# A two-layer fp32 decoder on one core: late weight columns and norm sums moved to VectorE, memsets, accumulating DMAs and casts queued elsewhere, two weight columns kept

## The chip, the cores and the metric

One core of a Trainium2 chip runs one launch of the kernel. The metric is the device time of that launch in microseconds. Lower is better. The kernel before was timed in three runs.

## What is computed

Two post-norm decoder layers over T = 528 tokens (16 learned ones ahead of 512 real ones), width 1024, hidden width 2816, all in float32. Cut to what matters:

```python
def hybrid_layer(h, ...):
    proj = einsum('bld,de->ble', h, w_in)
    ...                       # retention, multi-scale pooling, forgetting attention
    mix = concatenate([o_r, o_p, o_f], axis=-1)
    h = layer_norm(ALPHA * h + einsum('ble,ed->bld', mix, w_out), ln1_g, ln1_b)
    a, b = einsum('bld,df->blf', h, w1), einsum('bld,df->blf', h, w3)
    y = einsum('blf,fd->bld', silu(a) * b, w2)
    return layer_norm(ALPHA * h + y, ln2_g, ln2_b)
```

This is done twice, after a layer norm of the embedded input. There are thus two norms per layer; the text calls those after w_out the mixing norms (m0, m1 for layers 0 and 1) and the one after w2 of layer 0 the FFN norm (f0).

## The kernel before, in words

**Numbers.** Activations lie transposed, as 8 tiles of 128 features by tokens, and are cut by tokens into half A (272) and half B (256). Each float32 value is used as a rounded part `hi` and a rest `lo`, and a product is three matmuls into one PSUM accumulator: hi·hi, hi·lo, lo·hi (`mm3`, L236 to L240). There are two such accumulators (`acc`), so a matmul group can start when the group two before it has been read out of PSUM.

**Weights.** A chunk of 128x1024 is loaded by SP into one of 3 `raw` buffers (L167), cast to its hi part on ScalarE (L184), and its lo part is raw minus hi, by `sub_lo` (L141) on VectorE or on GpSimd (POOL). `ensure` (L174) does this; which engine does the subtraction is set chunk by chunk where `add_chunks` is called, by the table `CFG`: `o0` to `o7` for the eight column groups of w_out (each is streamed once for half A and once for half B), `i*` for w_in, `n*` for the first chunks of the FFN. L141 is also the line of every other hi/lo subtraction (the rest `xl` of the activations among them), so in the trace tiles tell them apart.

**Order.** TensorE's order is written by hand: `Plan` places pieces of matmuls by priorities and by a table `LAG` of latencies. The order of the other engines' queues comes from a scheduler; `tc.issue_after(ins)` puts what is issued inside it behind the instruction `ins` on its engine. Every queue is in order: an instruction that waits holds up all behind it.

**Norm** (L318 to about L400, `Norm`). `evac` adds the residual to a PSUM result (L332, VectorE), adds it to a running sum (L337), squares it (L341, ScalarE; the last one on VectorE, L339) and adds the square to a second running sum (L345). `CFG` s1 to s7 and t1 to t7 choose VectorE or POOL for the sums of L337 and L345. `stats` has TensorE transpose the sums (L359) and VectorE reduce them (L360); some small steps (L366 to L369, the power on POOL) give each token's scale, and L372 writes it into a diagonal matrix g. `apply` has TensorE spread g over partitions (L376), then, per tile of 128 features, VectorE subtracts the mean (L381) and multiplies by the scale (L382), ScalarE applies gain and bias (L312) and casts to `xh` (L314), and POOL subtracts to `xl` (L141). The first products after a norm take these tiles one by one. While one half is normed, TensorE works on the other half's last columns.

**FFN.** The first three hidden tiles are plain products (`ffn_hidden`: SiLU on ScalarE at L1164, times the second product on VectorE at L1186 in the first layer and L1243 in the last). The others use a seven-product scheme (`fast`), which needs sums of weight blocks and of activation blocks. `sums_of` (L191) makes the former: one SP load, two DMAs from POOL's queue that add on arrival (L197 into `s`, L198 into `raw`), two adds on VectorE (L207, L210) and casts. Its casts and VectorE work are placed behind marks set in the apply step; its two POOL DMAs are not. `factors` and `sums_of_x` (L1026 to L1064) make the latter into `Th` and `Tl`, with casts on ScalarE (L1043).

**w2 of layer 0** is used in two halves of the hidden width. In the second half, columns 4, 5 and 6 are used for half A first and loaded, cast and split a second time for half B, in the order 6, 5, 4 (`M2`).

**Mixing.** At the start of each mixing stage `clear` (L564) zeroes the states, and `forget` calls `causal` (L631), which writes the attention mask; all on POOL (L566 to L571, L634, L635).

## Time and profile before

| | |
|---|---|
| median of 3 runs | 1247.58 us (1243.88 to 1247.93) |
| the profiled execution | 1246.58 us |
| its span | 1244.8 us, 23626 instructions |
| DMA | 153.34 MB, mean 123 GB/s |

The span is the time between the first and the last instruction of the profiled execution; the execution's own time is 1.8 us more. Busy time is per engine: PE is TensorE's matmuls, PEld its weight loads, DVE VectorE, ACT ScalarE, POOL GpSimd. PEclk is the clock TensorE was granted as a share of 2.4 GHz; 0.50 is its lower level, 1.2 GHz. In a timeline, a row is start, duration, engine, line, operation, out<-in, shape and count, and in brackets how long the engine had been idle and what ended that. Where like instructions follow one another on an engine, one row holds them with their count, and its time runs from the first one's start to the last one's end.

### The profile page before, as it was taken

What the parts mean: (1) busy time and instruction counts of PE and PEld (TensorE: products, weight loads), DVE (VectorE), ACT (ScalarE), POOL (GpSimd) and SP (SyncE); (2) the same over time, 40 slices, a digit from 0 to 9 for tenths busy, and PEclk for the clock granted to TensorE, in tenths of its full rate; (3) what the DMA queues carried; (4) which work ended last, traced back from release to release, by engine and by line L of the source; (5) the groups of instructions that cost most, each with busy time, mean ns of one, the idle gap of its engine ahead of it and who ended that gap; (6) DMA issues with size and microseconds to landing.
All of it is one profiled execution on the core that took longest, in us unless ns stands there. A gap on an engine that the chain in (4) does not pass through costs nothing. (4 is left out here: it accounts for less than half of the span.)

```text
span 1244.8 us, 23626 instructions
## 1 busy us (share of the span) xinstructions
PE 1193.6 (96%) x9154; PEld 1142.3 (92%) x9154; DVE 844.5 (68%) x1732; ACT 603.7 (49%) x1182; POOL 374.9 (30%) x417
## 2 busy tenths in 40 slices
PE   7999999889999999999989899999999999999996
PEld 6999989879999999999989799998899999998885
DVE  6575687899885268864674755779887777762327
ACT  5436554456563246653354265444655555552221
POOL 5423348650110011101264243386511111100004
PEclk9999999999999999999989999998999999999999
DMA  6331212454862367722443221124468777633221
GB/s 236 114 102 64 70 35 68 153 144 119 212 165 82 102 189 182 178 77 78 128 149 125 82 73 56 48 86 152 136 160 205 176 187 177 156 102 102 85 101 68
DMA packets 59520, 153.34 MB, mean 123 GB/s; under 512 B 8392, under 2 KB 17128, under 8 KB 59408
## 3 DMA queue, kind: packets, MB, share of 16 engines
q1 hardware_dynamic: 48464, 131.90, 33.2%
q0 software_dynamic: 10944, 19.93, 9.9%
q8 instruction: 72, 1.18, 0.4%
q14 instruction: 40, 0.33, 0.1%
HBM read 145.83 MB, written 2.10 MB: 119 GB/s over the span
## 5 line engine op out<-in xcount | busy, mean ns | idle before, releaser
L238 PE MATMUL acc<-xh,w 128*128 128x256 f32 (+1 forms) x1024 | 303.0, 296 | 11.4 <-DVE ka L141 5.0
L239 PE MATMUL acc<-xl,w 128*128 128x256 f32 (+1 forms) x1024 | 294.4, 288 | 5.4 <-POOL xl L141 4.7
L240 PE MATMUL acc<-xh,w 128*128 128x256 f32 (+1 forms) x1024 | 293.7, 287 | 0.0
L141 DVE TENSOR_TENSOR w<-raw,w 128x1024 fp32r<-128x1024 f32 (+3 forms) x234 | 225.7, 984 | 67.4 <-ACT w L184 63.5
L184 ACT CAST w<-raw 128x1024 fp32r<-128x1024 f32 (+1 forms) x184 | 182.5, 993 | 163.1 <-PE acc L240 104.0
L238 PEld LDWEIGHTS acc<-xh,w 128*128 128x128 f32 x1024 | 196.8, 192 | 16.0 <-issue 6.1
L239 PEld LDWEIGHTS acc<-xl,w 128*128 128x128 f32 x1024 | 197.0, 192 | 7.5 <-POOL xl L141 6.3
L240 PEld LDWEIGHTS acc<-xh,w 128*128 128x128 f32 x1024 | 196.6, 192 | 0.0
L141 POOL TENSOR_TENSOR w<-raw,w 128x256 fp32r<-128x256 f32 (+1 forms) x70 | 111.3, 1595 | 76.4 <-ACT w L184 70.1
L198 POOL DMA_DIRECT2D raw<-in_w x38 | 32.8, 864 | 329.0 <-DMA raw<-in_w 102.9
L1141 PE MATMUL acc<-xh,w 128*128 128x264 f32 (+1 forms) x608 | 121.8, 283 | 0.0
L1141 PEld LDWEIGHTS acc<-xh,w 128*128 128x128 f32 x608 | 98.6, 188 | 0.2 <-ACT g L1099 0.2
L1141 PE MATMUL acc<-xl,w 128*128 128x264 f32 (+1 forms) x304 | 85.4, 281 | 0.0
L141 DVE TENSOR_TENSOR S<-sr,S 128x512 fp32r<-128x512 f32 x76 | 52.4, 689 | 47.3 <-ACT S L209 46.6
L299 POOL TENSOR_TENSOR r<-r,mhalf 128x1 f32<-128x1 f32 (+3 forms) x18 | 14.7, 821 | 185.4 <-DVE r L298 185.4
L1141 PE MATMUL acc<-Th,w 128*128 128x264 f32 (+1 forms) x304 | 61.2, 284 | 0.0
L1141 PE MATMUL one<-Th,S 128*128 128x264 f32 (+1 forms) x304 | 61.1, 283 | 0.0
L1141 PE MATMUL one<-xh,S 128*128 128x264 f32 (+1 forms) x304 | 60.9, 283 | 0.0
L1141 PE MATMUL acc<-Th,S 128*128 128x264 f32 (+1 forms) x304 | 60.9, 283 | 0.0
L1141 PE MATMUL one<-xh,w 128*128 128x264 f32 (+1 forms) x304 | 60.2, 282 | 0.0
L1141 PEld LDWEIGHTS acc<-xl,w 128*128 128x128 f32 x304 | 57.2, 188 | 0.0
L197 POOL DMA_DIRECT2D s<-in_w x38 | 37.8, 1002 | 61.5 <-DVE g L1243 12.3
(492 smaller groups left out, 3139.3 us busy)
## 6 DMA issues: line engine op xcount, KB each, us to landing
raw<-in_w SPq DMA_DIRECT2D x88, 512.0 KB, 4.1
raw<-in_w_in SPq DMA_DIRECT2D x42, 512.0 KB, 4.1
raw<-in_w_out SPq DMA_DIRECT2D x32, 512.0 KB, 3.4
raw<-in_w2b SPq DMA_DIRECT2D x22, 512.0 KB, 3.5
s<-in_w SPq DMA_DIRECT2D x38, 256.0 KB, 3.7
s<-in_w POOLq DMA_DIRECT2D x38, 256.0 KB, 6.4
raw<-in_w POOLq DMA_DIRECT2D x38, 256.0 KB, 5.4
raw<-in_w2a SPq DMA_DIRECT2D x19, 512.0 KB, 3.5
```

The costliest lines, as they stand in the source:

```text
L141: return eng.tensor_tensor(lo, full, hi.bitcast(F32), op=ALU.subtract)
L184: nc.scalar.copy(w[:, 0, :n], raw[:, :n])
L197: nc.gpsimd.dma_start(r1, src2[:, b], accum_op=ALU.add)
L198: nc.gpsimd.dma_start(a2[:, a], src1[:, a], accum_op=ALU.add)
L238: nc.tensor.matmul(ps, lhsT=wh, rhs=hi, start=first, stop=False)
L239: nc.tensor.matmul(ps, lhsT=wh, rhs=lo, start=False, stop=False)
L240: nc.tensor.matmul(ps, lhsT=wl, rhs=hi, start=False, stop=last)
L299: nc.gpsimd.tensor_tensor(r[:np_, :nb], r[:np_, :nb], mhalf[:np_, :nb], op=ALU.pow)
L1141: nc.tensor.matmul(ps, lhsT=a[:, w], rhs=b, start=fresh and k == 0 and q == 0, stop=k == 3 and q == 2, skip_group_check=True)
```

## The change

1. **w_out.** The lo part of a chunk is now made on POOL only for half A's columns with `o*` set except the last (0, 1, 3, 4, 6) and for columns 3 and 4 of half B. Column 7 of half A and columns 0, 1, 6 and 7 of half B go to VectorE: five subtractions per layer.
2. **Sums.** `s1`, `s5`, `t1` and `t4` of `CFG` go from 1 to 0, so every running sum is on VectorE: 4 additions per half of each norm, 24 in all.
3. **Queues.** A new helper `behind` places instructions behind the latest apply step's last mark on VectorE ("v"), ScalarE ("s") or, newly, POOL ("p", the last `xl`). Behind "p" come the memsets of `clear` and the mask of `causal` (in layer 1; in layer 0 there is no mark yet); behind all three the whole of `sums_of`, its POOL DMAs included; behind "s" the casts to `Th`.
4. **Plan.** `LAG` T goes from 16 to 4, and the sums of activations depend on other pieces.
5. **w2.** In the second half of the hidden width, the split columns 5 and 6 are kept (tile `wheld`, in the place of `Th` and `Tl`, which are free by then) and used again for half B; only column 4 is loaded a second time. That takes away four SP loads (1.44 MB), four casts and four subtractions.

The lines of `LAG` and `CFG` are left out of the diff.

```diff
-M2 = (0, 1, 2, 3, 4, 5, 6, 7, 6, 5, 4)
...
@@ -175,11 +174,16 @@
         while len(loaded) < len(chunks) and len(loaded) <= upto:
             fetch(len(loaded))
             raw, (_, n, eng) = raws[len(loaded)], chunks[len(loaded)]
-            w = wp.tile([P, 2, 1024], F32R, tag="w", name="w")
+            if eng in ("Th", "Tl"):
+                if n == 1024:
+                    wf[eng] = wf["pool"].tile([P, 2, KH * P], F32R, tag=eng, name="wheld")
+                w, eng = wf[eng][:, :, 1024 * (n < 1024):], nc.vector
+            else:
+                w = wp.tile([P, 2, 1024], F32R, tag="w", name="w")
             if eng == "S2":
                 c = len(loaded)
-                with ExitStack() as gates:
-                    loaded.append(sums_of(raws[c - 1], raw, loaded[-1], w, chunks[c - 1][0], chunks[c][0], gates))
+                with behind("v", "s", "p"):
+                    loaded.append(sums_of(raws[c - 1], raw, loaded[-1], w, chunks[c - 1][0], chunks[c][0]))
                 continue
             nc.scalar.copy(w[:, 0, :n], raw[:, :n])
             if eng != "S1":
@@ -188,7 +192,7 @@
                         sub_lo(e, w[:, 1, c0:c1], raw[:, c0:c1], w[:, 0, c0:c1])
             loaded.append(w)
 
-    def sums_of(a1, a2, w1, w2, src1, src2, gates):
+    def sums_of(a1, a2, w1, w2, src1, src2):
 
 
         a, b = slice(0, 512), slice(512, 1024)
@@ -200,8 +204,6 @@
         s1, s2 = (wf["pool"].tile([P, 2, 512], F32R, tag="S", name="S", bufs=3) for i in range(2))
         s4 = wf["pool"].tile([P, 2, 512], F32R, tag="S4", name="S4", bufs=2)
         v = nc.vector
-        for e in "vs":
-            gates.enter_context(tc.issue_after(marks["apply", e].ins))
         sub_lo(v, w1[:, 1, a], a1[:, a], w1[:, 0, a])
         nc.scalar.copy(s1[:, 0], r1)
         v.tensor_tensor(r2, r1, a1[:, a], op=ALU.add)
@@ -221,7 +223,7 @@
     for l in range(DEPTH):
         win_u.append([add_chunks(d["w_in"][l, m], 1024, quarters if l == 0 and m < CFG["pw"] else (None, nc.gpsimd, nc.vector)[CFG[f"i{m}"]] if l and m < 4 else None)
                       for m in range(N_IN)])
-        wout_u.append({h: [add_chunks(d["w_out"][l, m], 1024, nc.gpsimd if CFG[f"o{m}"] else nc.vector)
+        wout_u.append({h: [add_chunks(d["w_out"][l, m], 1024, nc.gpsimd if CFG[f"o{m}"] and m != 7 and (h == "A" or m in (3, 4)) else nc.vector)
                            for m in range(KD)] for h in "AB"})
         w13_u.append([])
         for fs, cut in ((KH, slice(0, KH * P)), (KF, slice(KH * P, DFF))):
@@ -229,7 +231,8 @@
                 w13_u[l].append(add_chunks(d["w13"][l, f], 1024, f"S{1 + f % 2}" if f >= 2 * HEAD else
                                            nc.gpsimd if f < 4 and CFG[f"n{f}"] else nc.vector))
             if l < DEPTH - 1:
-                w2_u.append([add_chunks(d["w2a"][m][:, cut], KH * P, nc.vector) for m in M2[:KD if fs < KF else None]])
+                w2_u.append([add_chunks(d["w2a"][m][:, cut], KH * P, f"T{'hl'[m - 5]}" if m in (5, 6) and fs == KF else nc.vector)
+                             for m in (*range(KD), 4)[:KD if fs < KF else None]])
         if l == DEPTH - 1:
             w2_u.append([add_chunks(d["w2b"][k], 1024, nc.vector) for k in range(KF)])
 
@@ -312,8 +315,16 @@
         nc.scalar.activation(out=y, in_=y if src is None else src, func=AF.Identity,
                              scale=pv[:, gc:gc + 1], bias=pv[:, bc:bc + 1])
         ins = nc.scalar.copy(x[0], y)
-        sub_lo(nc.gpsimd, x[1], y, x[0])
+        marks["apply", "p"] = sub_lo(nc.gpsimd, x[1], y, x[0])
         return ins
+
+    def behind(*engines):
+
+        st = ExitStack()
+        for e in engines:
+            if ("apply", e) in marks:
+                st.enter_context(tc.issue_after(marks["apply", e].ins))
+        return st
 
     class Norm:
 
@@ -562,13 +573,14 @@
         state = [ap_.tile([P, 2, 192], F32, tag=f"state{i}", name=f"state{i}") for i in range(2)]
 
         def clear():
-            for t in state:
-                nc.gpsimd.memset(t, 0.0)
-            nc.gpsimd.memset(vbd, 0.0)
-            for t in qb:
-                nc.gpsimd.memset(t[64:66].bitcast(F32), 1.0)
-            for m in range(2):
-                nc.gpsimd.memset(pu[m][:, :NM], 0.0)
+            with behind("p"):
+                for t in state:
+                    nc.gpsimd.memset(t, 0.0)
+                nc.gpsimd.memset(vbd, 0.0)
+                for t in qb:
+                    nc.gpsimd.memset(t[64:66].bitcast(F32), 1.0)
+                for m in range(2):
+                    nc.gpsimd.memset(pu[m][:, :NM], 0.0)
 
         vraw = {}
 
@@ -643,7 +655,8 @@
             nc.scalar.activation(out=a, in_=a, func=AF.Exp, scale=-1.0)
             nc.scalar.activation(out=a, in_=a, func=AF.Ln, bias=1.0)
             nc.vector.tensor_scalar(b, fl, 0.0, None, op0=ALU.min)
-            causal()
+            with behind("p"):
+                causal()
             nc.vector.tensor_tensor_scan(fl, a, b, 0.0, op0=ALU.add, op1=ALU.subtract)
             for i in range(2):
                 F["c", i] = ap_.tile([6, T], F32R, tag="tmp", name="flp", bufs=7)
@@ -1040,7 +1053,8 @@
         for (p, c0, c1), (q, _, _) in zip(second(k), second(k + 4)):
             v.tensor_tensor(t[2][:, c0:c1], q, p, op=ALU.subtract)
         for i in range(3):
-            nc.scalar.copy(Th[:, k, i], t[i])
+            with behind("s"):
+                nc.scalar.copy(Th[:, k, i], t[i])
             sub_lo(v, Tl[:, k, i], t[i], Th[:, k, i])
 
         def fourth():
@@ -1059,9 +1073,9 @@
         def make(k):
             later[k] = factors(k, n, hs, o, Th, Tl)
 
-        ps = [plan.add(lambda k=k: make(k), 0.0, [units[k // 2], ready], 5) for k in range(4)]
+        ps = [plan.add(lambda k=k: make(k), 0.0, [units[k], ready], 5) for k in range(4)]
         end = plan.add(lambda: [later[k]() for k in range(4)], 0.0, ps + [units[-1]], 5)
-        ps[0].holds("y", 3, units[3])
+        ps[0].holds("y", 3, ps[-1])
         return [(ps[-1], LAG["T"]), end]
 
     PRODUCTS = dict(P1=("A11", "B11", 0), P5=("s1", "T1", 1), P6=("s2", "T2", 0), P7=("s3", "T3", 0), P2=("A12", "B21", 2),
@@ -1173,8 +1187,8 @@
         base = 16 + l * PV_L
         N = T // 2
         wf["pool"] = gp
-        Th = gp.tile([P, 4, 3, N], F32R, name="Th")
-        Tl = gp.tile([P, 4, 3, N], F32R, name="Tl")
+        Th = gp.tile([P, 4, 3, N], F32R, tag="Th", name="Th")
+        Tl = gp.tile([P, 4, 3, N], F32R, tag="Tl", name="Tl")
         gt = {}
 
         def split(f, c0, c1, t):
@@ -1200,7 +1214,7 @@
         for f in range(HEAD):
             for h in "AB":
                 done[(f, 0), h].holds("y", 1, done[(f, 1), h])
-        deps = sums_of_x(N, hs, 0, Th, Tl, [done[u, "B"] for _, u in us], ready["B", KD - 1][0])
+        deps = sums_of_x(N, hs, 0, Th, Tl, [done[us[i][1], h] for i, h in ((0, "B"), (0, "B"), (4, "A"), (4, "B"), (5, "B"))], ready["B", KD - 1][0])
         gdone = {f: [(done[(f, 1), h], LAG["g"]) for h in "AB"] for f in range(HEAD)}
         prev = done[us[-1][1], "B"]
         dn = {}
@@ -1216,16 +1230,20 @@
             last = fast(l, fs[0 if i else HEAD:], 0, N, Th, Tl, yslot, lambda f: (yslot(N), yslot(N)), gated, deps, prev)
             gdone.update({f: [(p, LAG["g2"])] for f, p in last.items()})
             end = [last[fs[-1]]]
-            us = list(zip(w2_u[i], M2))
+            us = list(zip(w2_u[i], (*range(KD), 4)))
+            if i:
+                us[8:] = us[6], us[5], us[8]
             for part, halves in ((us[:4], "AB"), (us[4:7], "A"), (us[7:8], "AB"), (us[8:], "B")) if i else ((us, "AB"),):
                 dn.update(stage(part, lambda half, fs=fs: {f: tuple(g[:, :NA] if half == "A" else g[:, NA:] for g in gt[f]) for f in fs},
                                 list(fs), lambda h, key: n_of[h],
                                 lambda m, half, ps, i=i: norm[half].evac(m, ps) if i else evac2(m, half, ps),
                                 lambda half, key, k, end=end: gdone[k] + end, halves=halves, ahead=1 if i else 2, k0=fs[0]))
+                if len(part) == 1:
+                    plan.add(lambda: ensure(w2_u[1][8][1]), 0.0, [dn[7, "B"]], 8)
             end = [dn[us[-1][1], h] for h in "AB"]
         xn, nready = {}, {}
         for half in "AB":
-            ap = norm[half].finish([dn[m, half] for m in (range(KD) if half == "A" else M2[:4] + M2[7:])], base + 16, base + 24, xn)
+            ap = norm[half].finish([dn[m, half] for m in (range(KD) if half == "A" else (0, 1, 2, 3, 7, 6, 5, 4))], base + 16, base + 24, xn)
             ap.append(plan.add(lambda half=half: free(keep[half]), 0.0, [ap[-1]], 0))
             for k in range(KD):
                 nready[half, k] = (ap[-2], norm[half].lag["ap"] + 0.85 * k)
@@ -1248,7 +1266,7 @@
         for f in range(HEAD):
             for h in "AB":
                 done[(f, 0), h].holds("y", 1, done[(f, 1), h])
-        deps = sums_of_x(NB, hw, NM, Th, Tl, [done[u, "B"] for _, u in us], ready["B", KD - 1][0])
+        deps = sums_of_x(NB, hw, NM, Th, Tl, [done[us[i][1], h] for i, h in ((0, "B"), (0, "B"), (4, "A"), (4, "B"), (5, "B"))], ready["B", KD - 1][0])
         last = fast(l, range(HEAD, KF), NM, NB, Th, Tl, yslot, lambda f: (g[f][:, :NB], g[f][:, NB:]), lambda f, j, g: None, deps, done[us[-1][1], "B"])
         ht = {}
```

TensorE's queue holds the same matmuls in the same order as before, save that some read `wheld`. VectorE has 30 instructions more, POOL 34 fewer, ScalarE and SP 4 fewer each.

**Place 1: VectorE at the norm of half A after w_out, layer 0.** Here `w<-raw,w` is the lo part of a w_out chunk and the rows with `c_ident` write the diagonal. Before:

```order
L141 TENSOR_TENSOR w<-raw,w 128x1024
L372 TENSOR_SCALAR y<-c_ident,r 128x16
L372 TENSOR_SCALAR y<-c_ident,r 128x128 x2
L381 TENSOR_TENSOR y<-y,one 128x272 x2
L332 SCALAR_TENSOR_TENSOR y<-y,acc 128x256
L337 TENSOR_TENSOR y<-y 128x256
L382 TENSOR_TENSOR y<-y,one 128x272
```

And now:

```order
L140 TENSOR_TENSOR w<-raw,w 128x1024
L383 TENSOR_SCALAR y<-c_ident,r 128x16
L383 TENSOR_SCALAR y<-c_ident,r 128x128 x2
L348 TENSOR_TENSOR y<-y 128x256
L392 TENSOR_TENSOR y<-y,one 128x272 x2
L356 TENSOR_TENSOR y<-y 128x256
L343 SCALAR_TENSOR_TENSOR y<-y,acc 128x256
L140 TENSOR_TENSOR w<-raw,w 128x1024
L393 TENSOR_TENSOR y<-y,one 128x272 x2
```

What stands ahead of the diagonal is the same; behind it there are two running sums and a w_out subtraction that POOL did before. From the diagonal to the last multiplication by the scale, VectorE now has four w_out subtractions (before none) and four more running sums.

**Place 2: ScalarE and VectorE at the first hidden tiles after that norm, layer 0.** `Th` are the casts of activation sums, L1164 (now L1178) is the SiLU; L1186 (now L1200) is the product that reads an accumulator. ScalarE before, then now:

```order
L1164 ACTIVATE y<-acc 128x256
L1043 CAST Th<-y 128x264 x4
L184 CAST w<-raw 128x1024
L1043 CAST Th<-y 128x264 x2
L1182 CAST g0h<-y 128x256
L184 CAST w<-raw 128x1024
L1043 CAST Th<-y 128x264 x2
L1164 ACTIVATE y<-acc 128x256
```

```order
L1178 ACTIVATE y<-acc 128x256
L1057 CAST Th<-y 128x264 x4
L188 CAST w<-raw 128x1024
L1057 CAST Th<-y 128x264 x2
L1178 ACTIVATE y<-acc 128x256
```

The second SiLU of half B stood behind eight casts of `Th` and stands behind six now. VectorE before, then now, in the same place:

```order
L382 TENSOR_TENSOR y<-y,one 128x256 x2
L207 TENSOR_TENSOR sr<-s_3782,raw 128x512
L210 TENSOR_TENSOR sr<-sr,raw 128x512
L1186 TENSOR_TENSOR y<-y,acc 128x272
L141 TENSOR_TENSOR g1l<-y,g1h 128x272
```

```order
L393 TENSOR_TENSOR y<-y,one 128x256 x2
L1200 TENSOR_TENSOR y<-y,acc 128x272
L140 TENSOR_TENSOR g1l<-y,g1h 128x272
...
L140 TENSOR_TENSOR Tl<-y,Th 128x264
L209 TENSOR_TENSOR sr<-s_3782,raw 128x512
L1200 TENSOR_TENSOR y<-y,acc 128x256
```

The weight sum L207 (now L209) no longer stands ahead of half A's product; it stands directly ahead of the next product of half B.

**Place 3: POOL at the norm of half A after w2, layer 0.** Before, then now:

```order
L141 TENSOR_TENSOR xl<-y,xh 128x272 x4
L141 TENSOR_TENSOR w<-raw,w 128x256
L566 MEMSET state_7848 128x384
L566 MEMSET state_7849 128x384
L567 MEMSET vbd 96x384
L569 MEMSET qb_7838 2x256
L569 MEMSET qb_7839 2x256
L141 TENSOR_TENSOR xl<-y,xh 128x272
L571 MEMSET pu_7844 128x16
L571 MEMSET pu_7845 128x16
L634 MEMSET mask 128x528
L141 TENSOR_TENSOR w<-raw,w 128x256
```

```order
L380 TENSOR_TENSOR r<-r,mhalf 128x3
L140 TENSOR_TENSOR w<-raw,w 128x256
L140 TENSOR_TENSOR xl<-y,xh 128x272 x6
L140 TENSOR_TENSOR w<-raw,w 128x256
L140 TENSOR_TENSOR xl<-y,xh 128x272 x2
L380 TENSOR_TENSOR r<-r,mhalf 128x2
L601 TENSOR_TENSOR y<-y,rcs 128x272
L140 TENSOR_TENSOR xl<-y,xh 128x256 x8
L578 MEMSET state_7826 128x384
```

The memsets and the mask stood between the subtractions of `xl`; now they follow the last `xl` of half B, and two quarter chunks of w_in stand among half A's eight.

## Rows read from the trace of the kernel before

**Rows 1.** The page, busy time of the engines.

```profile
PE 1193.6 (96%) x9154; PEld 1142.3 (92%) x9154; DVE 844.5 (68%) x1732; ACT 603.7 (49%) x1182; POOL 374.9 (30%) x417
```

**Rows 2.** Windows: stretch, length, busy per engine (instructions), PEclk, DMA share, GB/s.

```profile
220.00:300.00 80.00, 69.83 (x529) 67.55 (x528) 71.37 (x142) 41.99 (x83) 38.53 (x34) 0.96 0.44 132
300.00:620.00 320.00, 320.00 (x2621) 319.79 (x2621) 209.29 (x382) 152.38 (x279) 39.28 (x42) 1.00 0.53 139
620.00:645.00 25.00, 20.25 (x139) 19.31 (x139) 19.03 (x37) 13.10 (x25) 17.08 (x23) 0.86 0.64 210
850.00:915.00 65.00, 56.96 (x433) 55.43 (x432) 55.22 (x112) 33.67 (x69) 31.42 (x30) 0.92 0.48 138
242.84:246.25 3.41, 3.41 (x17) 3.30 (x16) 3.06 (x10) 2.03 (x5) 0.77 (x1) 0.50 0.49 154
908.44:911.85 3.41, 3.41 (x18) 3.41 (x17) 2.79 (x9) 0.38 (x1) 0.00 (x0) 0.50 0.57 127
200.00:260.00 60.00, 56.13 (x433) 55.05 (x432) 52.71 (x76) 33.29 (x58) 45.32 (x34) 0.97 0.41 137
```

**Rows 3.** TensorE's waits, 220 to 300: us in total, times, longest.

```profile
PE one L376 <- DVE y L372: 5.4, 2, 3.4
PE acc L238 <- DVE y L1186: 2.5, 1, 2.5
PE acc L238 <- ACT y L1164: 1.4, 1, 1.4
```

**Rows 4.** TensorE's waits, 620 to 645.

```profile
PE acc L239 <- POOL xl L141: 4.7, 3, 2.2
```

**Rows 5.** TensorE's waits, 850 to 915.

```profile
PE one L376 <- DVE y L372: 4.4, 2, 2.8
PE acc L238 <- ACT y L1164: 2.5, 1, 2.5
PE one L359 <- DVE y L345: 1.2, 1, 1.2
```

**Rows 6.** Timeline of VectorE, 219 to 262.

```profile
219.72 0.43 DVE L345 TENSOR_TENSOR y<-y 128x272 f32<-128x272 f32 x1
...
229.34 2.55 DVE L345 TENSOR_TENSOR y<-y 128x272 f32<-128x272 f32 x1
...
237.95 1.23 DVE L141 TENSOR_TENSOR w<-raw,w 128x1024 fp32r<-128x1024 f32 x1 [1.47 <-ACT w L184]
239.09 3.24 DVE L372 TENSOR_SCALAR y<-c_ident,r 128x16 f32<-128x16 f32 x3
...
251.98 0.78 DVE L382 TENSOR_TENSOR y<-y,one 128x272 f32<-128x272 f32 x2
```

**Rows 7.** Timeline of POOL, 229 to 261.

```profile
229.21 2.38 POOL L141 TENSOR_TENSOR w<-raw,w 128x1024 fp32r<-128x1024 f32 x1 [2.19 <-ACT w L184]
...
239.72 2.33 POOL L141 TENSOR_TENSOR w<-raw,w 128x1024 fp32r<-128x1024 f32 x1
...
257.51 2.79 POOL L141 TENSOR_TENSOR xl<-y,xh 128x272 fp32r<-128x272 f32 x3
```

**Rows 8.** All runs of line L372: ns of one, minimum, median, maximum.

```profile
L372 DVE TENSOR_SCALAR y<-c_ident,r x14: 234/284/2434, 239.1 to 885.3; 128x128 f32<-128x128 f32 x12, 128x16 f32<-128x16 f32 x2
```

**Rows 9.** Timeline of POOL, 629 to 637.

```profile
633.80 1.47 POOL L141 TENSOR_TENSOR xl<-y,xh 128x272 fp32r<-128x272 f32 x1
635.23 1.27 POOL L635 TENSOR_SCALAR_AFFINE_SELECT mask<-mask 128x128 f32<-128x128 f32 x1
```

**Rows 10.** Timeline of VectorE, 272 to 280.

```profile
273.02 5.67 DVE L207 TENSOR_TENSOR sr<-s,raw 128x512 f32<-128x512 f32 x1
```

**Rows 11.** Timeline of POOL, 272 to 280.

```profile
272.29 5.84 POOL L141 TENSOR_TENSOR xl<-y,xh 128x256 fp32r<-128x256 f32 x8
```

**Rows 12.** Timeline of ScalarE, 274 to 276.

```profile
274.65 0.70 ACT L314 CAST xh<-y 128x256 fp32r<-128x256 f32 x2
```

**Rows 13.** Tile s, 255 to 310: the adding DMAs' landing.

```profile
DMA to landing us min/median/max: 5.1/7.7/8.1
```

More of the change, by code (lines that the diff above doesn't have):

```diff
@@ L35 @@
 PV_L = 40
-LAG = dict(T=16.0, g2=3.0, y2=2.0, q=1.5, kb=4.25, fb=3.21, q_1=1.5, kb_1=5.0, fb_1=3.45, rot=8.62, vt=2.86, kt=3.84, kv=1.23, kvo=2.5, rs=2.5, ro=6.35, rp=0.69, f=12.8, a=5.62, b=0.77, v0=9.72, k=3.2, s=0.99, p=2.78, pt=1.24, mt=2.77, u=5.1, rm=3.74, pm=3.74, mx=3.25, y=0.8, st=2.25, ap=2.42, g=2.1, ga=8.46, gn=6.42, gt=21.89, gs=0.33, gs2=0.86, gl=2.0, w=10.8, rot_1=10.43, vt_1=1.2, kt_1=6.88, kv_1=0.74, kvo_1=1.6, rs_1=4.5, ro_1=7.28, rp_1=0.48, f_1=11.9, k_1=1.95, s_1=1.7, p_1=2.78, pt_1=1.16, mt_1=2.85, u_1=6.42, rm_1=3.0, pm_1=3.72, mx_1=3.17, y_m0A=0.8, y2_m0A=4.1, st_m0A=5.7, ap_m0A=2.42, y_m0B=1.6, y2_m0B=2.5, st_m0B=2.2, ap_m0B=2.42, y_f0A=0.8, y2_f0A=2.0, st_f0A=3.75, ap_f0A=2.42, y_f0B=2.5, y2_f0B=3.5, st_f0B=3.52, ap_f0B=2.42, y_m1A=0.8, y2_m1A=4.2, st_m1A=5.5, ap_m1A=2.42, y_m1B=1.6, y2_m1B=2.5, st_m1B=2.2, ap_m1B=3.15)
@@ L39 @@
-CFG = dict(h0=2, h1=1, h2=0, h3=2, h4=1, h5=2, h6=1, h7=2, g0=2, g1=1, g2=0, g3=0, g4=0, g5=2, g6=2, g7=1, p0=1, p1=0, p2=0, p3=0, p4=0, p5=0, p6=0, p7=0, q0=0, q1=1, q2=0, q3=1, q4=0, q5=1, q6=0, q7=1, pw=2, a3=7, a4=5, e1=7, e2=7, ws=1, wf=0, i0=2, i1=0, i2=0, i3=2, o0=1, o1=1, o2=0, o3=1, o4=1, o5=0, o6=1, o7=1, n0=0, n1=0, n2=0, n3=0, s1=1, s2=0, s3=0, s4=0, s5=1, s6=0, s7=0, t1=1, t2=0, t3=0, t4=1, t5=0, t6=0, t7=0)
+LAG = dict(T=4.0, g2=3.0, y2=2.0, q=1.5, kb=4.25, fb=3.21, q_1=1.5, kb_1=5.0, fb_1=3.45, rot=8.62, vt=2.86, kt=3.84, kv=1.23, kvo=2.5, rs=2.5, ro=6.35, rp=0.69, f=12.8, a=5.62, b=0.77, v0=9.72, k=3.2, s=0.99, p=2.78, pt=1.24, mt=2.77, u=5.1, rm=3.74, pm=3.74, mx=3.25, y=0.8, st=2.25, ap=2.42, g=2.1, ga=8.46, gn=6.42, gt=21.89, gs=0.33, gs2=0.86, gl=2.0, w=10.8, rot_1=10.43, vt_1=1.2, kt_1=6.88, kv_1=0.74, kvo_1=1.6, rs_1=4.5, ro_1=7.28, rp_1=0.48, f_1=11.9, k_1=1.95, s_1=1.7, p_1=2.78, pt_1=1.16, mt_1=2.85, u_1=6.42, rm_1=3.0, pm_1=3.72, mx_1=3.17, y_m0A=0.8, y2_m0A=4.1, st_m0A=5.7, ap_m0A=2.42, y_m0B=1.6, y2_m0B=2.5, st_m0B=2.2, ap_m0B=2.42, y_f0A=0.8, y2_f0A=2.0, st_f0A=3.75, ap_f0A=2.42, y_f0B=2.5, y2_f0B=3.5, st_f0B=3.52, ap_f0B=2.42, y_m1A=0.8, y2_m1A=4.2, st_m1A=5.5, ap_m1A=2.42, y_m1B=1.6, y2_m1B=2.5, st_m1B=2.2, ap_m1B=3.15)
@@ L42, in mix_half @@
+CFG = dict(h0=2, h1=1, h2=0, h3=2, h4=1, h5=2, h6=1, h7=2, g0=2, g1=1, g2=0, g3=0, g4=0, g5=2, g6=2, g7=1, p0=1, p1=0, p2=0, p3=0, p4=0, p5=0, p6=0, p7=0, q0=0, q1=1, q2=0, q3=1, q4=0, q5=1, q6=0, q7=1, pw=2, a3=7, a4=5, e1=7, e2=7, ws=1, wf=0, i0=2, i1=0, i2=0, i3=2, o0=1, o1=1, o2=0, o3=1, o4=1, o5=0, o6=1, o7=1, n0=0, n1=0, n2=0, n3=0, s1=0, s2=0, s3=0, s4=0, s5=0, s6=0, s7=0, t1=0, t2=0, t3=0, t4=0, t5=0, t6=0, t7=0)
 def mix_half(c, qoff):
```

## The prediction

> **What bounds the kernel now.** I read the page first, then the windows of the stages, then TensorE's waits in the stretches that are not full, then the timelines of the engines it waits for. TensorE is busy 96% of the span and the next engine, VectorE, 68% [rows 1], so only what TensorE waits for or runs slowly can be won. The long dense stretch from 300 to 620 shows 320.00 of 320.00 us at full clock, with the DMA engines at 0.53 [rows 2]: nothing that only saves loads or casts there can shorten it. The losses that this change can reach lie at three norms: 220 to 300 (69.83 of 80 us busy, clock 0.96), 620 to 645 (20.25 of 25, 0.86) and 850 to 915 (56.96 of 65, 0.92) [rows 2]. There the waits are: the diagonal of the mixing norm (L372) 5.4 us and hidden products held up by L1186 and L1164 2.5 and 1.4 [rows 3]; the split tiles `xl` from POOL 4.7 [rows 4]; again the diagonal 4.4, L1164 2.5 and the running sum 1.2 [rows 5]. That is 9.3 + 4.7 + 8.1 = 22.1 us. Each group of waits is followed by a stretch at the lower clock level, 1.2 GHz; there are five in all, of which the first and the last are shown, each 3.41 us at 0.50 [rows 2]. Work done in 3.41 us there takes 1.7 at full clock, so the five cost 8.5. All that can be won here is about 30.6 us.
>
> **Why the waits are there.** A running sum takes 0.43 us, and 2.55 while POOL makes a w_out rest that takes 2.38 [rows 6, 7]: VectorE's instruction stood still until POOL's was done. The same happens at the diagonal. Its three instructions take 3.24 us, started at 239.09, while POOL runs a w_out rest from 239.72 for 2.33 [rows 6, 7]; the median of L372 is 0.284 and its longest 2.434 [rows 8]. At 273.02 the weight sum L207 takes 5.67 us under eight `xl` subtractions that hold POOL for 5.84 [rows 10, 11], and the hidden product L1186 queues behind it. At the FFN norm `xl` is simply late in POOL's queue.
>
> **The change, part by part** (against the profiled execution, 1246.6).
>
> *Diagonal, half A, both mixing norms.* VectorE's queue ahead of the diagonal is unchanged (its place in the order), so it still starts when the w_out rest at 237.95 is done. Without POOL's rest the three instructions take 3 x 0.28 = 0.9 instead of 3.24 [rows 6, 8]. The waits go from 3.4 to 0.9 and from 2.8 to 0.6, a gain of 2.5 and 2.2 [rows 3, 5]; with less idle time ahead of them I expect the low-clock stretch behind each to go, 1.7 each. Bounds: 0 if another POOL instruction takes the place of the rest, 3.4 and 2.8 plus 1.7 each at most. I take 4.2 + 3.9 = **8.1**.
>
> *What that costs in the apply step.* Between the diagonal and the last multiplication of half A VectorE now has four w_out rests and four sums more: 4 x 1.23 + 4 x 0.43 = 6.6 us, with about 0.4 more for a residual add that comes earlier, 7.0 in all. Against that it no longer stands still under POOL's rest in mid-step, some 2.0 by the pair of rows above (2.55 against 0.43), and starts 2.5 earlier. The last multiplication, which ended at 252.76, so comes about 2.5 later on the clock of the trace, while TensorE wants it 4.2 earlier. Before, the last `xl` came at 260.30 [rows 6, 7], 7.5 behind it, because POOL was busy with rests and sums. Unhindered the way from multiplication to `xl` is about 2.3 (affine, cast and a subtraction of 0.73, an eighth of 5.84 [rows 11]), so 5.3 of slack stands against 2.5 + 4.2 = 6.7: I take **-1.4** per mixing norm, **-2.8** for both. Bounds: 0, if VectorE's idle 7.3 of 60 us in this stretch [rows 2] falls where it helps; -4.2 each, if POOL's lag does not shrink.
>
> *Diagonal, half B.* Two w_out rests still stand ahead of its statistics. Only the sums get shorter. The waits are 5.4 - 3.4 = 2.0, and 1.6 + 1.2 = 2.8 [rows 3, 5]; gains lie between 0 and these, and since the subtractions ahead stay, I take a small part, 0.7 each, **1.4**.
>
> *First hidden tiles, layer 0.* L1186 no longer waits for the weight sum (2.5), the SiLU goes ahead of two casts (1.4) and a low-clock stretch goes (1.7): 5.6. New is that the adding DMAs now start behind the last `xl`. The last `xh` is cast at 275.35 [rows 12]; 0.73 for `xl` [rows 11], 5.1 to 8.1 for the landing [rows 13] and some 1.1 for the weight sum and the product behind it make 282.3 to 285.3 for the product of half B that now queues there. TensorE, with this stretch tightened, wants that accumulator at about 283. So the new wait is between 0 and 2.2, with 1.7 for the clock at the long end; I take 1.0, near the middle. **4.6.**
>
> *First hidden tiles, layer 1.* L1164's 2.5 and 1.7 of clock, less 0.5 for the same new wait in a smaller place: **3.7.** Bounds as above.
>
> *FFN norm.* Memsets and mask leave POOL's queue ahead of `xl`; the mask's selection alone is 1.27 us [rows 9]. Two w_in quarters stay between them, so I leave 0.5 of the 4.7 [rows 4] and add the clock, 1.7: **5.9.** Bounds 3 and 6.4. The memsets come later in front of w_in rests that are needed after half B's tiles; `xl` of half B covers them. If that cover is missing the cost is under the time of the memsets, and it is inside the range.
>
> *w2 columns.* Four loads, four casts and four subtractions less, all in or just behind the full stretch: **0**. The dense stage hides them, and the room they free in VectorE's and ScalarE's queues shows only at the FFN norm, counted there. The plan's table moves nothing on TensorE: 0.
>
> Sum: 8.1 - 2.8 + 1.4 + 4.6 + 3.7 + 5.9 = 20.9; 1246.6 - 20.9 = **1225.7 us**. The profiled execution is 1.0 under the median of the runs shown, 1247.58, well inside what is not known. The forecast's own range is 1217 to 1234, from the gains and losses of the apply step and the weight sum.
>
> **A rule and a row.** The rows say that a subtraction on POOL stops VectorE's two-operand work from SBUF, and by them a moved rest costs VectorE 1.23 us of work and takes away up to 2.1 of standing still. The Trainium skill ("SBUF — State Buffer", Who interferes with whom) gives the same block in both directions: the engine that starts first holds the shared port pair for the whole instruction and the other waits. By that rule the rests now on VectorE can hold up POOL's `xl`; one such is in the trace, 1.47 us instead of 0.73 [rows 9, 11]. By the rows alone I charge nothing more for it; if every one of four rests did so, each norm would lose up to 4 x 0.7 = 2.8 more where no slack is left, which the bound of -4.2 contains.
>
> **The rivals.**
>
> *The waits move (0.14).* The apply step pays its upper bound in both norms (2 x 2.8 = 5.6 more) and the weight sum its own (1.2 and 1.7). For it: VectorE is busy 52.71 of 60 us there [rows 2]. Against it: POOL's lag of 7.5 has a visible cause that is removed. 20.9 - 8.5 = 12.4, so 1234.2.
>
> *All of it goes (0.09).* Every wait and every low-clock stretch: 1246.6 - 30.6 = 1216.0. Against it: two w_out rests still stand ahead of half B's statistics.
>
> *Moving work between VectorE and POOL gives nothing (0.05).* A rest costs the pair of engines much the same on either, since one stands still for the other; the w_out and sum terms (8.1, -2.8, 1.4) vanish together and only the reordered queues remain: 5.9 + 4.6 + 3.7 = 14.2, 1232.4. The row for it is the sum at 2.55; against it, 1.23 us on VectorE is about half of 2.33 on POOL. The Trainium skill states this as a caution ("Perfetto Trace Analysis", Optimizing Scalar/DVE Operations): because GpSimd and VectorE share an SBUF read port, offloading between those two might not help.
>
> *No change (0.07).* The scheduler's order hardly shortens a wait on the chip, or each saved wait reappears at the next accumulator: about 1246.
>
> *Slower (0.05).* VectorE becomes the bound at the mixing norms. Each gets 5 x 1.23 + 8 x 0.43 = 9.6 us more work, and it idles only 7.3 us in 200 to 260 [rows 2]. If all 9.6 falls on the path at both, and the gains there do not come, the result is 19.2 - 14.2 = 5.0 slower, 1251.6. It decides from a loss of 7.1 per norm. Against it: 4 or more of VectorE's busy us there are standing still.
>
> **How the numbers follow.** My forecast has 0.60. A measurement of this kernel can tell about 0.3%, 3.7 us, from no change. Faster by more than that are the forecast, the moved waits, the full gain and the queues alone: 0.60 + 0.14 + 0.09 + 0.05 = 0.88. Within it 0.07, slower 0.05. The range of 1213 to 1240 leaves out no change, slower and a little of the tails.
>
> **What would show it.** In the changed profile, each L372 (now L383) about 0.3 us and no POOL row over it; no `xl` wait over 0.5 us near 620 to 645, and memsets behind half B's `xl`; L1186's product not behind the weight sum; at most two of the five stretches at 0.50; the dense stretch unchanged at 320 of 320. I am wrong if TensorE's first hidden products wait for `xl` of half A for several us, if POOL's `xl` rows lengthen to 1.5 us, or if the weight sum waits for its DMA so long that an accumulator does.

## The result and the profile after

The changed kernel takes 1227.45 us in the median (1225.67 to 1229.70, 4 runs), against 1246.58 before (1243.88 to 1247.93, 4 runs, one more than shown above). The ratio is 0.985, 95% interval 0.9825 to 0.9876. The profiled execution took 1226.59 us with a span of 1224.8, 20.0 less than before. The forecast was 1225.7.

The page's busy times, after:

```profile
PE 1187.4 (97%) x9154; PEld 1135.8 (93%) x9154; DVE 833.3 (68%) x1762; ACT 600.7 (49%) x1178; POOL 322.1 (26%) x383
```

The windows that answer to those of [rows 2] (length, busy per engine with instructions, PEclk, DMA share, GB/s), shifted by what had been won until then:

```profile
220.00:300.00 80.00, 74.41 (x593) 72.38 (x592) 71.00 (x161) 47.55 (x93) 25.83 (x26) 1.00 0.51 150
300.00:616.00 316.00, 315.69 (x2582) 315.26 (x2583) 206.95 (x385) 148.60 (x274) 31.95 (x35) 1.00 0.53 140
616.00:641.00 25.00, 24.20 (x193) 23.54 (x191) 20.70 (x49) 15.42 (x36) 13.46 (x18) 1.00 0.36 118
835.00:900.00 65.00, 61.75 (x502) 59.84 (x501) 58.22 (x123) 39.63 (x79) 25.27 (x25) 1.00 0.51 148
```

TensorE works at full clock in all three norms, where the granted clock was 0.96, 0.86 and 0.92, and the first of these windows holds 593 matmuls instead of 529. All five low-clock stretches at the norms are gone; one appeared elsewhere, in the second mixing stage:

```profile
684.40:687.90 3.50, 3.50 (x17) 3.50 (x16) 0.44 (x1) 0.21 (x1) 0.00 (x0) 0.51 0.91 262
```

TensorE's waits in 220 to 315 and then in 836 to 915, after (us in total, times, longest); they answer to [rows 3] and [rows 5]:

```profile
PE one L387 <- DVE y L383: 1.7, 2, 0.9
PE acc L241 <- DVE y L343: 1.4, 4, 0.4
PE acc L1155 <- ACT y L1105: 1.0, 1, 1.0
PE one L370 <- DVE y L348: 1.0, 1, 1.0
...
PE one L370 <- DVE y L348: 1.1, 1, 1.1
PE one L387 <- DVE y L383: 1.0, 1, 1.0
PE acc L1155 <- DVE xl L140: 0.8, 1, 0.8
```

The diagonal's 5.4 and 4.4 are 1.7 and 1.0, and the long waits for L1186 and L1164 do not occur. For L343, the residual add that empties an accumulator, there are now four waits of at most 0.4 us in m0 (before, one of 0.5). About 1 us for the running sum L348 is new in m0; in m1 it stands in the place of the 1.2 us for the sum L345. Near 616 to 641 no `xl` wait is left [rows 4].

**Where the 20 us came from.** Both traces hold 9154 matmuls in the same order, so the start of the same matmul can be compared, in us. Last column: what was won since the line above.

```
matmul   before    after    won in all   since the line above
     0     6.91     6.82       0.09
  1740   232.72   233.45      -0.73      -0.82  embedding, first mixing stage
  1812   246.61   243.33       3.28      +4.01  m0, diagonal of half A
  1912   259.38   257.50       1.88      -1.40  its apply step
  1956   267.98   265.64       2.34      +0.46  half B
  2112   293.58   285.26       8.32      +5.98  first hidden tiles
  2300   316.48   310.09       6.39      -1.93  first seven-product tile
  4860   629.06   622.67       6.39       0.00  dense stretch
  4944   648.42   633.76      14.66      +8.27  f0
  5100   667.80   654.53      13.27      -1.39  first mixing products behind it
  6540   853.06   840.42      12.64      -0.63  second mixing stage
  6612   867.53   849.93      17.60      +4.96  m1, diagonal of half A
  6704   878.33   862.49      15.84      -1.76  its apply step
  6744   886.68   870.13      16.55      +0.71  half B
  6930   913.29   892.37      20.92      +4.37  first hidden tiles
  7100   933.36   913.50      19.86      -1.06  first seven-product tile
  9153  1234.95  1215.19      19.76      -0.10  the rest
```

### The profile page after: what moved, and what is told of

It reads as the page before. It is cut to its first block, busy times and chain, and to the rows that moved or that the text cites. A ratio compares the mean times of both kernels' runs of the same rounds, so it can differ in the third digit from the quotient of the medians.

```text
span 1224.8 us, 23583 instructions
## 1 busy us (share of the span) xinstructions
PE 1187.4 (97%) x9154; PEld 1135.8 (93%) x9154; DVE 833.3 (68%) x1762; ACT 600.7 (49%) x1178; POOL 322.1 (26%) x383
## 5 line engine op out<-in xcount | busy, mean ns | idle before, releaser
L242 PE MATMUL acc<-xl,w 128*128 128x256 f32 (+1 forms) x1024 | 291.3, 284 | 0.4 <-DVE xl L905 0.4
L188 ACT CAST w<-raw 128x1024 fp32r<-128x1024 f32 (+1 forms) x176 | 176.1, 1002 | 153.9 <-PE acc L243 86.5
L241 PEld LDWEIGHTS acc<-xh,w 128*128 128x128 f32 x1024 | 194.1, 190 | 10.7 <-issue 5.7
L242 PEld LDWEIGHTS acc<-xl,w 128*128 128x128 f32 x1024 | 194.1, 190 | 1.4 <-DVE xl L905 0.6
L243 PEld LDWEIGHTS acc<-xh,w 128*128 128x128 f32 x1024 | 193.9, 189 | 0.0
L140 POOL TENSOR_TENSOR w<-raw,w 128x256 fp32r<-128x256 f32 (+1 forms) x60 | 88.3, 1478 | 94.1 <-ACT w L188 87.8
L1155 PEld LDWEIGHTS acc<-xh,w 128*128 128x128 f32 x608 | 98.5, 188 | 0.2 <-ACT g L1113 0.2
L140 POOL TENSOR_TENSOR xl<-y,xh 128x256 fp32r<-128x256 f32 (+1 forms) x57 | 48.3, 857 | 45.8 <-ACT xh L317 39.8
L1155 PEld LDWEIGHTS acc<-xl,w 128*128 128x128 f32 x304 | 57.2, 188 | 1.5 <-DVE xl L140 1.5
```

The costliest lines, as they stand in the source:

```text
L140: return eng.tensor_tensor(lo, full, hi.bitcast(F32), op=ALU.subtract)
L188: nc.scalar.copy(w[:, 0, :n], raw[:, :n])
L241: nc.tensor.matmul(ps, lhsT=wh, rhs=hi, start=first, stop=False)
L242: nc.tensor.matmul(ps, lhsT=wh, rhs=lo, start=False, stop=False)
L243: nc.tensor.matmul(ps, lhsT=wl, rhs=hi, start=False, stop=last)
L1155: nc.tensor.matmul(ps, lhsT=a[:, w], rhs=b, start=fresh and k == 0 and q == 0, stop=k == 3 and q == 2, skip_group_check=True)
```

## The experiments

Twelve kernels: the changed one with one part undone, the one before with one part alone or two, and one step further. "Trace" is the difference of the last matmul's start between two profiled executions, as in the table. A single execution is no average: where trace and median part, both are given. A gain in us behind a ratio is 1 minus the ratio, times the time before. Each edit also lets the scheduler order the queues anew, so the worth of a part includes that.

For the five kernels with a part undone at a loss, the medians lie 2.9 to 6.0 us above the changed kernel's, but each ratio's interval overlaps its 0.9825 to 0.9876. That the loss belongs to the part rests on the place where it appears in the trace, and on the runs that add the part to the kernel before.

**Rests and sums back on POOL.**

```diff
-nc.gpsimd if CFG[f"o{m}"] and m != 7 and (h == "A" or m in (3, 4)) else nc.vector
+nc.gpsimd if CFG[f"o{m}"] else nc.vector
...
-s1=0, s5=0, t1=0, t4=0
+s1=1, s5=1, t1=1, t4=1
```

> The changed kernel with its w_out rests and its running sums chosen as before (more of both on POOL); all else as changed. My theory: POOL's rests again stop VectorE at the diagonal, so TensorE's wait for it is again about 3 us at half A of both mixing norms and the terms 8.1 - 2.8 + 1.4 = 6.7 us go: about 1233. Rival (moving work between the two engines gives nothing): about 1227, with the diagonal's wait as short as in the changed kernel or its loss found again elsewhere.

Measured: 1230.34 us, ratio to before 0.9862 (0.9836 to 0.9888); by the ratio alone not told from the changed kernel, 2.9 us longer by the medians. In the trace 4.0 us are lost, where 6.7 were expected: 4.0 and 3.7 at the two diagonals, given back 1.2 and 1.0 in the apply steps and a little in half B. Timeline of VectorE, then of POOL, in this kernel:

```profile
239.63 3.24 DVE L383 TENSOR_SCALAR y<-c_ident,r 128x16 f32<-128x16 f32 x3
...
240.26 2.33 POOL L140 TENSOR_TENSOR w<-raw,w 128x1024 fp32r<-128x1024 f32 x1
```

It is the pair of [rows 6, 7] again, three instructions in 3.24 us. In the changed kernel no L383 takes more than 0.288:

```profile
L383 DVE TENSOR_SCALAR y<-c_ident,r x14: 228/280/288, 240.0 to 868.8; 128x128 f32<-128x128 f32 x12, 128x16 f32<-128x16 f32 x2
```

The rival that nothing is won between these two engines falls for rests and sums together; the next run shows that it is the rests.

**The sums alone back on POOL** (only the second pair of lines above).

> The changed kernel with s1, s5, t1 and t4 on POOL again; the w_out rests stay on VectorE. My theory: it was the rests (2.3 us each on POOL) that stopped the diagonal, the sums only add or take 0.4 us: within 1.5 us of the changed kernel, 1226 to 1229, the diagonal's wait at half A short. Rival (the sums on POOL hold VectorE as much): 3 to 4 us longer.

Measured: 1225.94 us, ratio 0.9827 (0.9799 to 0.9855); trace 0.7 us shorter than the changed kernel. On balance the sums bring nothing; what this part wins lies in the rests. By stage, with the sums on POOL the diagonal of m0 loses 0.4 us (its three instructions take 1.08 us beside a sum of 1.44 on POOL, where they took 3.24 beside a rest and 0.62 beside nothing), and the apply step of m0 gains 1.3 back; m1's apply step does not change.

**Memsets and mask free on POOL again.**

```diff
-            with behind("p"):
+            with ExitStack():
                 for t in state:
...
-            with behind("p"):
-                causal()
+            causal()
```

> The changed kernel with the memsets and the mask queued on POOL as before, in front of the split tiles of the FFN norm. My theory: TensorE waits again some 4 us for xl near 630 and the clock falls once: 5.9 us longer, about 1233. Rival (the kept w2 columns and the freed subtractions are what shortened this norm): at most 1.5 us longer, about 1228, no xl wait over 1 us there.

Measured: 1231.51 us, ratio 0.9857 (0.9832 to 0.9882); 4.1 us longer by the medians; trace 2.5 longer (this execution is the shortest of its runs), 5.2 lost up to matmul 4944 and 1.4 + 0.7 regained behind it, and 0.6 shorter ahead of it. Timeline of POOL, and then, in a fence of its own, TensorE's wait in 612 to 645:

```profile
622.28 0.78 POOL L578 MEMSET state<- 128x384 f32 x2 [1.52 <-PE acc L243]
...
625.36 3.18 POOL L140 TENSOR_TENSOR xl<-y,xh 128x272 fp32r<-128x272 f32 x2
```

```profile
PE acc L242 <- POOL xl L140: 3.3, 2, 2.3
```

The mechanism is the one predicted; the size is 2.5 to 4.1 of the 5.9 expected.

**The same part alone on the kernel before** (memsets and mask `behind("p")`, nothing else).

> The kernel before with one edit: memsets and mask behind the last xl on POOL. My prediction's term is 5.9 us, so 1242 against a before of about 1248. What the run with w2's columns loaded twice showed (its FFN norm lost 6.9 us although the memsets were out of the way) says less: the xl waits of 4.7 go, but TensorE then waits at half B's diagonal, whose VectorE work stands behind a w_in rest that is late; 0 to 2 us gained, 1246 to 1248.

Measured: 1246.33 us against 1246.11, ratio 0.9998 (0.9978 to 1.0018); trace 0.1. No gain of this part alone is told from 0; the interval reaches from 2.7 us won to 2.2 lost. In its trace f0 wins 1.1 us: with the memsets away TensorE still waits there, 2.4 us for `xl`, 0.8 for the diagonal and 0.6 for `xh`.

**w2's columns loaded twice again.**

```diff
-f"T{'hl'[m - 5]}" if m in (5, 6) and fs == KF else nc.vector) for m in (*range(KD), 4)
+nc.vector) for m in (*range(KD), 6, 5, 4)
...
```

> The changed kernel with columns 5 and 6 of w2 loaded, cast and split a second time as before. My theory: the stretch is full, 0 us, 1227 within 2. Rival (those four loads, casts and subtractions stand in the queues ahead of the FFN norm): 3 to 6 us longer, 1230 to 1233, with a wait near 620 to 640.

Measured: 1233.41 us, ratio 0.9882 (0.9859 to 0.9905); trace 6.1 longer: 9.1 lost at f0 up to matmul 4944, 2.1 regained behind it, 0.9 shorter ahead of it. Timelines of ScalarE, then of VectorE, then the window of the clock:

```profile
630.74 1.05 ACT L188 CAST w<-raw 128x1024 fp32r<-128x1024 f32 x1 [2.17 <-DMA raw<-in_w_in]
...
631.83 1.22 DVE L140 TENSOR_TENSOR w<-raw,w 128x1024 fp32r<-128x1024 f32 x1 [1.58 <-ACT w L188]
...
635.86 0.44 DVE L602 TENSOR_TENSOR y<-y,rcs 128x272 f32<-128x272 f32 x1 [2.53 <-DMA y<-y]
636.22 0.98 DVE L383 TENSOR_SCALAR y<-c_ident,r 128x128 f32<-128x128 f32 x2
```

```profile
635.72:642.54 6.82, 5.29 (x21) 5.11 (x22) 6.68 (x20) 1.91 (x5) 1.51 (x2) 0.50 0.02 6
```

The four loads are issued ahead of the first w_in chunks. The w_in cast waits 2.17 us for its DMA, VectorE's rest 1.58 for the cast, and half B's diagonal queues behind both and behind L602, which waits for a DMA of its own. That last wait, 2.53 us, ends last: SP issues this DMA from 629.74 on, behind later w_in loads, and from 626.61 on in the changed kernel, where L602 also stands behind the diagonal and not ahead of it. TensorE waits 3.7 us for L383 there, and 6.82 us at half clock begin in that wait.

**The same part alone on the kernel before.**

> The kernel before with one edit: w2 columns 5 and 6 of the second half kept for half B. My prediction's term is 0 us. What the run with the columns loaded twice showed says that these loads make the first w_in chunks late: then 3 to 5 us are gained here, 1243 to 1245, while the xl waits behind the memsets (some 3.5 us with the mask and the clock) stay.

Measured: 1240.95 us, ratio 0.9955 (0.9934 to 0.9977), 5.6 us; the profiled execution is the shortest of its runs, 8.1 by trace, of which 5.0 lie at f0 and the rest in stages that this edit does not touch. ScalarE's last `xh` cast of half A in the kernel before, then in this one:

```profile
633.34 0.41 ACT L314 CAST xh<-y 128x272 fp32r<-128x272 f32 x1
```

```profile
628.68 0.41 ACT L320 CAST xh<-y 128x272 fp32r<-128x272 f32 x1
```

Without the second load's casts between its affines, ScalarE ends the apply step 4.7 us earlier, though TensorE reaches the stage only 0.5 earlier. So this part acts through ScalarE's queue and through the DMA queue; the four VectorE subtractions that go with the loads were not tried apart. It is the larger part at f0: from matmul 4860 to 5100 the traces take 38.75 us before, 37.63 and 39.50 in the two kernels with the memsets away and the columns loaded twice, 33.78 and 35.63 in the two with the columns kept and the memsets in the way, and 31.87 after. Beside kept columns moving the memsets is thus worth 1.9 to 3.8 us here; with columns loaded twice, between a gain of 1.1 and a loss of 0.8, which is no more than single executions differ by there (38.32 to 41.98 in three further kernels with neither edit).

**The adding DMAs early again.**

```diff
-                with behind("v", "s", "p"):
-                    loaded.append(sums_of(...))
+                with ExitStack() as gates:
+                    loaded.append(sums_of(..., gates))
...
-    def sums_of(a1, a2, w1, w2, src1, src2):
+    def sums_of(a1, a2, w1, w2, src1, src2, gates):
...
+        gates.enter_context(behind("v", "s"))
         sub_lo(v, w1[:, 1, a], a1[:, a], w1[:, 0, a])
```

> The changed kernel with the adding DMAs of the weight sums free to be issued early, and only what follows them placed behind the marks of VectorE and ScalarE, as before. My theory: the weight sum stands again ahead of the hidden product and the two terms 4.6 + 3.7 = 8.3 us go, about 1235.5; a part less where the other edits to the casts help by themselves. Rival (the hidden products were held by the casts of Th, not by the weight sum): 1 to 3 us longer, about 1229, TensorE's wait for L1200 absent.

Measured: 1232.25 us, ratio 0.9874 (0.9851 to 0.9898); trace 4.6 longer, 2.3 at the first hidden tiles of layer 0, 0.7 at half B of m1, and 0.9 in the second mixing stage, which differs by as much between kernels that are alike there. Timeline of POOL and TensorE's wait in 265 to 300:

```profile
269.31 0.89 POOL L202 DMA_DIRECT2D raw<-in_w  x1 [4.80 <-DMA raw<-in_w]
```

```profile
PE acc L243 <- POOL xl L140: 1.4, 2, 0.9
```

POOL stands 4.80 us before it can issue the adding DMA, which waits for the load it adds to; half B's `xl` queue behind it. TensorE waits for those, not for the product of [rows 3]. The wait for L1200 is absent, as the rival said, but it is not the casts of `Th` that hold TensorE here, and the size lies between the two: neither the theory nor the rival had this place.

**The weight sums behind the apply step, alone on the kernel before** (the same edit the other way).

> The kernel before with one edit: the whole of the weight sums, POOL's adding DMAs included, behind the marks of the apply step. My prediction's terms are 4.6 + 3.7 less what the casts of Th bring, so 6 to 8 us, about 1241. Rival: the run with the adding DMAs early lost 4.6 us to xl waits and not to the product L1186; then the gain here is that of the xl queue, 3 to 5 us, 1243 to 1245.

Measured: 1246.43 us against 1246.11, ratio 1.0002 (0.9983 to 1.0020). The profiled execution is the longest of its runs, 1250.91; its rows show why the expected gain did not come. Timeline of ScalarE and TensorE's wait in 280 to 300:

```profile
287.69 0.41 ACT L1049 CAST Th<-y 128x264 fp32r<-128x264 f32 x1 [2.56 <-DVE y L1047]
288.01 0.38 ACT L1170 ACTIVATE y<-acc 128x256 f32<-128x256 f32 x1
```

```profile
PE acc L236 <- ACT y L1170: 3.3, 1, 3.3
```

The product comes earlier, and TensorE runs into the SiLU L1170, which queues behind casts of `Th` that wait for VectorE. In layer 1 the same wait is 3.7 us.

**Casts of `Th` and plan as before** (in the changed kernel).

```diff
-            with behind("s"):
-                nc.scalar.copy(Th[:, k, i], t[i])
+            nc.scalar.copy(Th[:, k, i], t[i])
```

with `LAG` T at 16 and the dependences of the activation sums as before (these lines are left out here).

> The changed kernel with the casts to Th free again and the plan's dependences and latency of the activation sums as before; the weight sums stay behind the apply step. My theory: the weight sums alone gained nothing because the second SiLU then waits behind those casts (3.3 and 3.7 us in that run); so here TensorE waits again for L1178 some 3 us at the first hidden tiles of each layer, with the clock 5 to 8 us longer, 1232 to 1235. Rival (the reordering of casts and plan is of no consequence): within 1 us of the changed kernel.

Measured: 1231.40 us, ratio 0.9878 (0.9851 to 0.9905); 4.0 us longer by the medians; trace 5.9 longer: 2.4 lost at the first hidden and seven-product tiles of layer 0 and 4.4 at those of layer 1, 0.9 shorter ahead of them. The wait for the SiLU is back, 3.3 and 3.7 us.

**Both hidden-tile edits together on the kernel before.**

> The kernel before with two edits together: weight sums behind the apply step, and casts to Th and plan of the activation sums as in the changed kernel. The prediction's terms 4.6 + 3.7 = 8.3 us belong to this pair: about 1238 against 1246. If the two edits are worth no more together than alone: 1244 to 1246.

Measured: 1239.16 us against 1245.48, ratio 0.9943 (0.9920 to 0.9965), 7.1 us; trace 8.3. The weight sums alone bring nothing; as a pair the two bring about what the prediction gave them. The casts and the plan alone were not run on the kernel before, but the changed kernel with the adding DMAs early is the changed kernel without the weight sums' edit. Over the first hidden and seven-product tiles of both layers (matmuls 1956 to 2300 and 6744 to 7100) the traces take 94.1 to 95.2 us in the four kernels with neither edit, 96.8 with the weight sums alone, 94.6 in the changed kernel without the casts and the plan, 90.2 in the changed kernel without the weight sums, 87.8 with both. So the casts and the plan keep more than half of the gain without the weight sums, and the weight sums none without them.

**Rests and sums alone on the kernel before.**

> The kernel before with one edit: w_out rests and running sums as in the changed kernel. My prediction's terms 8.1 - 2.8 + 1.4 = 6.7 us gained, 1241. The run with this part undone lost 3.9 us, with the apply step's loss at 0.6 to 1.5 per norm: by that 3 to 5 us are gained, 1243 to 1245. Rival (moving work between the two engines gives nothing): 1248.

Measured: 1241.51 us, ratio 0.9968 (0.9954 to 0.9982), 4.0 us; trace 5.0, with 3.9 and 4.8 at the diagonals and losses of 1.4 and 1.8 in the apply steps.

The three parts that gain by themselves on the kernel before, this one, the kept columns and the pair, add up to 4.0 + 5.6 + 7.1 = 16.7 of the 18.7 us that the ratio 0.985 stands for; the rest is of the size of the memsets beside kept columns.

**One step further: rests behind the diagonal.**

```diff
-                self.mark = nc.vector.tensor_scalar(...)
+                self.mark = marks["sums"] = nc.vector.tensor_scalar(...)
```

> The changed kernel, in which the weight rests that VectorE makes after a norm's sums are placed behind the diagonal instead of behind the last running sum. In the changed kernel two such rests (2.35 us) stand ahead of half B's statistics and TensorE waits 0.9 to 1.0 us there at each norm. If that delay is what remains, 1 us is gained at each mixing norm and the time is 1225 to 1226; if the rests are then late for the hidden products, or in the way of the multiplications, it is the same or up to 4 us longer.

Measured: 1224.88 us (1223.03 to 1225.70), ratio 0.9824 (0.9796 to 0.9851). It beats the kernel before. Against the changed kernel the intervals of the ratios overlap; the trace is 1.9 us shorter: 1.3 won at half B of each mixing norm and up to 1.0 at other places, with losses of up to 1.1 elsewhere. Timeline of VectorE at half B of m0:

```profile
261.74 0.48 DVE L383 TENSOR_SCALAR y<-c_ident,r 128x128 f32<-128x128 f32 x2 [0.81 <-POOL r L380]
262.13 1.22 DVE L140 TENSOR_TENSOR w<-raw,w 128x1024 fp32r<-128x1024 f32 x1
```

The diagonal now waits for POOL's small step only, and TensorE's wait for it at half B is gone.

## Why the prediction held, and where it did not

The time, 1227.45, lies 1.75 us from the forecast. Part of that nearness is luck: two terms have the right size for a reason that the runs do not bear out. By the table, term by term:

- *Diagonals*, 8.1: measured 4.0 + 5.0 = 9.0. Right, with the cause shown by the first experiment: the wait returns with POOL's rest. The 5.0 at m1 is too much for the change. The prediction took each of the five low-clock stretches as 3.41 us, but two last twice as long, one at f0 and one here (windows, before):

```profile
635.37:642.20 6.83, 5.90 (x23) 5.40 (x24) 1.82 (x4) 0.39 (x1) 2.60 (x3) 0.50 0.64 219
860.65:867.48 6.83, 6.06 (x26) 5.88 (x27) 6.70 (x16) 4.19 (x9) 2.79 (x2) 0.50 0.30 106
```

The four other kernels whose POOL rest falls on this diagonal have one of 3.41 us there and take 12.94 to 13.24 us over the stage, against 14.47 in the trace before and 9.51 after; 3.7, as in the first experiment, is nearer. In the kernel with the hidden-tile pair alone, POOL's rest starts at 856.36, when the diagonal (855.55, 0.95 us) is all but done: the stage takes 9.48, and the apply step behind it 14.43 instead of 10.80. And a low-clock stretch costs a little less than half its length: matmuls on 256 columns start 0.213 us apart in it and 0.118 at full clock, so 3.41 us of them cost 1.5 (an estimate) and not the 1.7 of the sum.

- *Apply steps*, -2.8: measured -1.4 - 1.8 = -3.2. The size was right, the place was not. I had TensorE wait for a late `xl`, so that the size agrees is luck. It waited for accumulators (at m0, four waits of up to 0.4 us for L343, which stands behind rests and sums on VectorE) and for the running sum. At m0 the loss is that of the sums: 1.3 of its 1.4 come back with the sums alone on POOL (0.9 net of what the diagonal ahead then loses). At m1 they bring nothing back, and rests and sums together 1.0 of the 1.8. One sign that I had named for being wrong did show, without its consequence: three of the sixteen `xl` in these two apply steps take 1.56 to 2.06 us, and TensorE waits for none of them. POOL mostly waits for ScalarE's `xh` instead of making anyone wait:

```profile
248.70 0.82 POOL L140 TENSOR_TENSOR xl<-y,xh 128x272 fp32r<-128x272 f32 x1 [0.89 <-ACT xh L317]
```

- *Half B*, 1.4: 0.5 + 0.7 = 1.2. The two rests ahead of the statistics were indeed what stayed, as the last experiment showed by moving them.
- *First hidden tiles*, 4.6 and 3.7: 6.0 - 1.9 = 4.1 and 4.4 - 1.1 = 3.3. The new loss came a step later than I put it. The weight sum's DMA was in time; its sum and the product behind it take 0.69 and 0.41 us without a wait:

```profile
279.08 0.69 DVE L209 TENSOR_TENSOR sr<-s,raw 128x512 f32<-128x512 f32 x1
279.68 0.41 DVE L1200 TENSOR_TENSOR y<-y,acc 128x256 f32<-128x256 f32 x1
```

The loss is at the first seven-product tile, where TensorE waits 1.0 us for L1105. It comes with the pair of edits (1.9 and 1.1 also in the kernel with the pair alone), and L1105 stands on ScalarE behind a cast of the weight sums, L211, before which the engine idles 1.58 us; what that cast waits for the profile does not show. And I had added the two edits as separate gains: the weight sums are worth nothing without the casts and the plan.
- *FFN norm*, 5.9: 8.3 - 1.4 = 6.9. Near in size, wrong in its cause, so this nearness too is luck. The step that failed is **"w2 columns: 0"**, together with giving the whole term to the memsets. Memsets and mask alone bring nothing that can be told from 0 (0.9998), the kept columns alone 5.6, and by the traces the memsets are worth something (1.9 to 3.8 at f0) only with the columns kept. I had looked at the full stretch in which the loads are issued, and not at the queues that they fill for the next one: ScalarE's casts between the affines of f0, and the w_in loads behind them.
- *Not in the sum*: -0.8, -0.6 and -0.1, together -1.5. The first is within the spread: in the fourteen traces that stage takes 225.5 to 227.1 us, both ends in variants of the changed kernel. The second mixing stage, where the moved memsets now stand, takes 184.2 to 186.9 in them, 185.3 before and 185.9 after; that too is within the spread.

Of the rivals, "moving work between the two engines gives nothing" is half true: the sums bring nothing, the rests some 4. Here the Trainium skill's caution ("Perfetto Trace Analysis", Optimizing Scalar/DVE Operations) holds for the sums and not for the rests, which blocked a step that TensorE waits for. "Slower" failed because VectorE's busy time in 220 to 300 hardly changed (71.37 before, 71.00 after) although it ran 161 instructions there instead of 142: the work added replaced standing still.
